# A hybrid decoder layer on one core: ordering edges for the less urgent work, four weight units split again in every tile, and the first rests on the vector engine

## The chip, the cores and the metric

The kernel runs on one core of one Trainium2 chip. The metric is the device time of one execution in microseconds; the time before is the median of three executions. Beside them one execution was profiled, and every duration below comes from that one. "Lands" means that a transfer has completed: the profile shows for each transfer when it was issued and, for most, when it landed.

## The reference, cut to what matters

The layer normalises x (2048 rows of 1024), projects it with one wide matrix, runs three kinds of head on the result, gates them, projects back, normalises and adds x.

```python
h = rms_norm(x, pre_norm_g)
proj = h @ w_in                      # 2816 columns
a_u, a_v, sq, sk, sv, mq, z = jnp.split(proj, split_at, axis=-1)
y_a = chunked_spatial_gating(gelu(a_u), gelu(a_v), ...)      # chunks of 128 rows
y_b = sliding_window_attention(sq, sk, sv, attn_sinks, rel_bias)
mk, mv = jnp.split(rms_norm(mem, mem_norm_g) @ w_mem_kv, 2, axis=-1)
y_c = memory_cross_attention(mq, mk, mv)                     # 256 memory rows
y = concatenate([y_a, y_b, y_c], axis=-1) * silu(z)
x = x + rms_norm(y @ w_out, post_norm_g)
```

Everything is float32. The kernel keeps that precision on TensorE by splitting each operand into a rounded high part and the rest, and summing three products (high by high, high by rest, rest by high).

## The kernel before, in words

**Split.** The function `split(hi, lo, src)` is the pair of instructions that the whole change is about: ScalarE (ACT) rounds `src` into `hi`, then VectorE (DVE), or for some weights GpSimd (POOL), writes the rest `src - hi` into `lo`. It is used on weights, on the normalised input and on attention probabilities.

**Tiles and units.** The 2048 rows are worked in four tiles of 512 (t = 0 to 3). In each tile TensorE (PE) runs through 22 weight units of 1024 rows by 128 columns (34 loads in all with the memory projection), 24 matmuls of 128x512 each: four units V (0 to 3), SV (4), K (5), two Q (6, 7), two MQ (8, 9), then the gate units Z (10 to 17) and U (18 to 21). A unit stands in a tile `whl` (high parts and rests, 1 MB, four buffers). Its raw weights come into `wraw` (512 KB, three buffers); the same three buffers also hold `wo_...` and `ya_...` blocks for the output projection. Once a unit has been split, it can be stored to a DRAM tensor `split_d`, and later tiles then load the ready 1 MB from there in place of loading and splitting. The table `stored_at` says in which tile a unit is stored: before, the V units are split in tiles 0 and 1 and stored in tile 1; SV, K and Q are split in tiles 0, 1 and 2 and stored in tile 2; all others are stored in tile 0.

**The end of a tile.** While PE runs the last units of tile t, the next tile's input is made: `make_h` scales a 128x512 block of x (`xj` or `xk`) on DVE and splits it into `hT`, eight blocks k = 0 to 7 in all. Unit V0 needs blocks 0 and 1, V1 blocks 2 and 3, and so on. `next_stats` squares x on ACT (`xs`) for the norm. In the same stretch the eight memory-attention pieces (named c_h_cc) end: PE transposes probabilities into `tp_c`, `split` turns them into `pT_c`, PE multiplies them into `o_c`, ACT copies half of it to `oh_c` and DVE adds both into `OC`. The gates run through `sc_z`, `Z_z`, `e_u`, `G_u` and `a`.

**What sets the order.** PE's order and that of the queue that issues the transfers (SP) are written out by hand. The orders of ACT, DVE and POOL are chosen at build time by a scheduler from its own estimate; on the chip each engine then works strictly in that order, so whatever stands behind a waiting instruction waits too. `tc.issue_after(x)` adds an edge: what is inside comes behind x on its engine. Before, `make_h`, the squares and the pieces in `aside` stand behind the latest exponentials and products of an attention piece (`late["exp"]`, `late["product"]`). In tile 3 `first_sums` reads four `ya` blocks (named 11, 21, 22 and 12), combines them and stores two sums `sd_S`.

**PSUM.** Attention pieces and the gating product `sg` share four buffers (`ps_t`): PE can begin a new one only when an earlier one has been read.

Of the kernel before, what the change touches and what calls it, by code (L numbers as in the profile page):

```python
# [11 lines left out]
AF = mybir.ActivationFunctionType  # L12
ALU = mybir.AluOpType
AX = mybir.AxisListType

P = 128
# [3 lines left out]
TS = 512  # L20
NT = SEQ // TS
# [4 lines left out]
GELU_C = math.sqrt(2.0 / math.pi)  # L26
# [4 lines left out]
U_V, U_SV, U_K, U_Q, U_MQ, U_Z, U_U, U_O, U_MK, U_MV = 0, 4, 5, 6, 8, 10, 18, 22, 30, 32  # L31
# [16 lines left out]
def kernel(  # L48
# [16 lines left out]
    nc = tc.nc  # L65
# [16 lines left out]
    def f32(ap):  # L82
        return ap.bitcast(F32)
# [1 line left out]

    aside = []

    def split(hi, lo, src, lo_engine=None):
        nc.scalar.copy(hi, src)  # L89
        (lo_engine or nc.vector).tensor_tensor(lo, src, f32(hi), ALU.subtract)  # L90


    order = []
# [33 lines left out]
    def split_unit(i):  # L127
        u, t = order[i]
        w = wp.tile([P, 2, D], F32R, tag="whl", name=f"whl_{t}_{u}")
        ready[u, t] = w  # L130
        if i not in raws:
            nc.sync.dma_start(f32(w), wo_d[u][t] if u in wo_d else split_d[u])
            return
        raw = raws.pop(i)
        if t == 0 and u in BEHIND:

            aside.append([lambda: split(w[:, 0], w[:, 1], raw), lambda: pending.discard(u)])
            pending.add(u)
# [76 lines left out]
    def next_stats(t):  # L215

        r = {}
        parts = tiny.tile([P, 2, 4], F32, tag="ss2", name=f"ss2_{t}")  # L220

        def load(n):
            i, c = divmod(n, 2)
            r[n] = sp.tile([P, TS], F32, tag="xk", name=f"xs_{t}_{n}", bufs=2)
            rows = x[t * TS : (t + 1) * TS].rearrange("(p i) d -> p i d", i=4)
            nc.sync.dma_start(r[n], rows[:, i, c * 512 : c * 512 + 512])

        def square(n):
            i, c = divmod(n, 2)

            with tc.issue_after(late["exp"].ins):
                nc.scalar.activation(r[n], r[n], AF.Square, accum_out=parts[:, c, i : i + 1])
# [30 lines left out]
    def first_h(xk, k):  # L263

        g = g_pre[:, k : k + 1]
        hT = hTs[0]
        nc.scalar.mul(hT[:, 0, k, :], xk, g)
        nc.vector.scalar_tensor_tensor(hT[:, 1, k, :], xk, g, f32(hT[:, 0, k, :]), ALU.mult, ALU.subtract)  # L268


# [10 lines left out]

    def make_h(t, k):
        hT, xk = hTs[t % 2], raw_x.pop(k)

        with tc.issue_after(late["exp"].ins), tc.issue_after(late["product"].ins):
            nc.vector.scalar_tensor_tensor(xk, xk, g_pre[:, k : k + 1], late["bcs", t], ALU.mult, ALU.mult)
            split(hT[:, 0, k, :], hT[:, 1, k, :], xk)

# [159 lines left out]


    def queue_aside(scalar, vector):  # L450
        late["product"] = vector
        with tc.issue_after(scalar.ins), tc.issue_after(vector.ins):
            for f in aside.pop(0) if aside else ():
                f()

    def window_unit(t, c, S, O, done):
# [25 lines left out]
            nc.vector.tensor_tensor(Lc[:, hs, :P], L[:, :, 0:P], L[:, :, P:], ALU.max)  # L482
        nc.vector.tensor_reduce(nm, Lc[:, :, : P + 1], axis=AX.X, op=ALU.max, negate=True)  # L483
        for h in range(4):
            last = late["exp"] = nc.scalar.activation(Lc[:, h, : P + 1], Lc[:, h, : P + 1], AF.Exp, bias=nm[:, h : h + 1],  # L485
                                        accum_out=den[:, h : h + 1])
        nc.vector.reciprocal(den, den)
        queue_aside(last, nc.vector.tensor_tensor(Lc[:, :, :P], Lc[:, :, :P],
# [3 lines left out]
        for h in range(4):  # L492
            nc.tensor.transpose(tp[:, h, :], Lc[:, h, :P], ident)
        own = sp.tile([P, 2, 4, P], F32R, tag="pT", name=f"po_{tag}")
        split(own[:, 0], own[:, 1], tp)
        if not first:

            prev = sp.tile([P, 2, 4, P], F32R, tag="pT", name=f"pp_{tag}")
# [20 lines left out]
    def memory_unit(t, h, cc, S, O, done):  # L519

        tag = f"c{t}_{h}_{cc}"
        lg = ps_t.tile([P, 2, 256], F32, tag="t", name=f"l_{tag}")
        for e in range(2):
            q0 = (2 * cc + e) * P
            for s in range(2):
                nc.tensor.matmul(lg[:, e, :], S[:, h % 2, q0 : q0 + P], MK[:, h, s, :],
                                 start=(s == 0), stop=(s == 1))
        p = sp.tile([P, 2, 256], F32, tag="L", name=f"L_{tag}", bufs=4)
        nm = tiny.tile([P, 2], F32, tag="nm", name=f"nm_{tag}", bufs=4)
        den = tiny.tile([P, 2], F32, tag="den", name=f"den_{tag}", bufs=4)  # L530
        nc.vector.tensor_reduce(nm, lg, axis=AX.X, op=ALU.max, negate=True)  # L531
        if t == 0:
            nc.vector.tensor_tensor(nm, nm, late["rstd"][:, 2 * cc : 2 * cc + 2], ALU.mult)
        for e in range(2):
            scale = late["rstd"][:, 2 * cc + e : 2 * cc + e + 1] if t == 0 else 1.0
            last = late["exp"] = nc.scalar.activation(p[:, e, :], lg[:, e, :], AF.Exp, bias=nm[:, e : e + 1], scale=scale,  # L536
                                        accum_out=den[:, e : e + 1])
        nc.vector.reciprocal(den, den)
        queue_aside(last, nc.vector.tensor_tensor(p, p, den[:, :, None].broadcast_to([P, 2, 256]), ALU.mult))
        yield  # L540
        tp = ps_t.tile([P, 2, 256], F32, tag="t", name=f"tp_{tag}")
        for j in range(2):
            for e in range(2):
                nc.tensor.transpose(tp[:, j, e * P : (e + 1) * P], p[:, e, j * P : (j + 1) * P], ident)
        pT = sp.tile([P, 2, 2, 256], F32R, tag="pT", name=f"pT_{tag}")
        split(pT[:, 0], pT[:, 1], tp)
        yield
        o = ps_t.tile([P, 256], F32, tag="t", name=f"o_{tag}")
        for n, (s, j) in enumerate(((0, 0), (0, 1), (1, 0), (1, 1))):
            nc.tensor.matmul(o, MV[:, j, h].rearrange("p a b -> p (a b)"), pT[:, s, j, :], start=(n == 0), stop=(n == 3))  # L550
        oh = sp.tile([64, 256], F32, tag="oh", name=f"oh_{tag}", bufs=1)
        nc.scalar.copy(oh, o[64:128, :])
        r0 = 64 * (h % 2)
        nc.vector.tensor_tensor(O()[r0 : r0 + 64, h // 2, 2 * cc * P : 2 * (cc + 1) * P], o[0:64, :], oh, ALU.add)
        done()

    def gelu2(ps, tag, out_tag, bufs):

        e = sp.tile([P, TS], F32, tag="e", name=f"e_{tag}", bufs=3)
        nc.scalar.activation(e, ps, AF.Square, scale=math.sqrt(GELU_A))  # L560
        nc.vector.scalar_tensor_tensor(e, e, 1.0, ps, ALU.add, ALU.mult)
        nc.scalar.activation(e, e, AF.Tanh, scale=GELU_C)
        G = sp.tile([P, TS], F32, tag=out_tag, name=f"G_{tag}", bufs=bufs)
        nc.vector.scalar_tensor_tensor(G, e, 1.0, ps, ALU.add, ALU.mult)
        return G

    def silu2(ps, tag, out_tag, bufs):

        G = sp.tile([P, TS], F32, tag=out_tag, name=f"Z_{tag}", bufs=bufs)
        nc.scalar.activation(G, ps, AF.Tanh, scale=0.5)  # L570
        nc.vector.scalar_tensor_tensor(G, G, 1.0, ps, ALU.add, ALU.mult)
        return G


# [657 lines left out]
```

## Time and profile before

| | |
|---|---|
| median of 3 executions | 775.2 us (772.15 to 775.22) |
| profiled execution | 776.51 us, of which 774.7 us are the span from its first to its last instruction |
| mean granted TensorE clock | 0.991 |
| PE busy | 758.9 us (98%) |
| DVE, ACT, POOL busy | 565.4, 394.0, 119.8 us |
| bytes moved | 200 MB, mean 259 GB/s |

The times of PE's matmuls overlap, since they are pipelined: the step from one start to the next is what counts, 0.227 us for a 128x512 one when nothing is late. So a busy share of 98% doesn't say that PE lost only 2%: it can be busy and slow. A row of the timeline merges like instructions in a run; its first number is the start in us, its second the time from the first start to the last end, and brackets hold the idle time before it and what ended that.

### The profile page before, as it was taken

The page shows a single profiled execution, that of the slowest core. Times are in us where ns is not written, and L with a number is a line of the kernel's source. Part 1 is how long each engine was busy: PE and PEld are TensorE (multiplying, and loading weights), DVE is VectorE, ACT ScalarE, POOL GpSimd, SP SyncE. Part 2 cuts the span into 40 slices and gives each one's busy share as a digit, 9 for nine tenths or more (in the row PEclk, how much of TensorE's full clock was granted, in tenths as well). Part 3 has the DMA queues.
Part 4 walks back from the last instruction along what each step waited for, and adds up shares of the span by engine and source line. Part 5 has one row for each costly group of instructions (what it writes and reads, how often), then busy time and mean ns, then how long its engine had stood idle before and what let it go on. Part 6 is the DMA issues. An engine that isn't in the chain of part 4 may idle for free. (4 is left out here: it accounts for less than half of the span.)

```text
span 774.7 us, 10625 instructions
## 1 busy us (share of the span) xinstructions
PE 758.9 (98%) x3764; PEld 639.3 (83%) x3764; DVE 565.4 (73%) x1064; ACT 394.0 (51%) x877; POOL 119.8 (15%) x125
## 2 busy tenths in 40 slices
PE   9999999989999999999999999999999999999995
PEld 7878988868888888888878888888888888888884
DVE  6496899885748889854589796647986415885787
ACT  7786776633645656246365552544444233443441
POOL 4555221000202300001023000101310000020012
PEclk9999999989999999999999999999999999999998
DMA  8856388768377898737999988774474699937618
GB/s 328 299 185 243 130 304 312 255 218 325 137 272 272 278 316 313 276 135 222 349 348 298 332 281 326 263 281 162 137 227 157 217 383 399 379 111 274 245 47 306
DMA packets 54709, 200.27 MB, mean 259 GB/s; under 512 B 5595, under 2 KB 6144, under 8 KB 44416
## 3 DMA queue, kind: packets, MB, share of 16 engines
q1 hardware_dynamic: 54128, 198.99, 72.3%
q8 instruction: 30, 0.49, 0.3%
q10 hardware_dynamic: 528, 0.59, 0.2%
q14 instruction: 23, 0.19, 0.1%
HBM read 142.93 MB, written 56.64 MB: 258 GB/s over the span
## 5 line engine op out<-in xcount | busy, mean ns | idle before, releaser
L301 PE MATMUL g_z<-hT,whl 128*128 128x512 f32 x768 | 195.3, 398 | 0.0
L301 PEld LDWEIGHTS g_z<-hT,whl 128*128 128x128 f32 x768 | 139.5, 190 | 25.3
L301 PE MATMUL g_u<-hT,whl 128*128 128x512 f32 x384 | 97.7, 396 | 0.0
L719 PE MATMUL v<-whl,hT 128*128 128x512 f32 x384 | 89.1, 392 | 0.4 <-DVE hT L268 0.3
L719 PEld LDWEIGHTS v<-whl,hT 128*128 128x128 f32 x384 | 72.1, 189 | 16.6 <-DVE hT L268 0.8
L301 PEld LDWEIGHTS g_u<-hT,whl 128*128 128x128 f32 x384 | 69.2, 188 | 12.7
L89 ACT CAST whl<-wraw 128x1024 fp32r<-128x1024 f32 (+1 forms) x39 | 39.9, 1026 | 35.7 <-DMA wraw<-in_wst 10.3
L173 POOL TENSOR_TENSOR rsr_v<-rsa_v,mhalf 128x4 f32<-128x4 f32 x16 | 16.8, 1056 | 223.3 <-DVE mv L744 202.7
L301 PE MATMUL g_q<-hT,whl 128*128 128x512 f32 x192 | 45.9, 394 | 0.0
L500 POOL TENSOR_SCALAR_AFFINE_SELECT pp_b<-po_b 128x512 fp32r<-128x512 f32 x30 | 20.8, 694 | 157.3 <-ACT po_b L89 157.3
L301 PE MATMUL g_mq<-hT,whl 128*128 128x512 f32 x192 | 44.7, 389 | 0.0
L1083 PE MATMUL Y_S<-hT,yop_S 128*128 128x512 f32 x192 | 44.2, 389 | 0.0
L1083 PE MATMUL Y<-hT,yop 128*128 128x512 f32 x192 | 43.8, 389 | 0.0
L988 POOL TENSOR_TENSOR r<-a,mhalf 128x1 f32<-128x1 f32 x16 | 13.5, 845 | 191.2 <-DVE a L986 185.1
L1083 PEld LDWEIGHTS Y<-hT,yop 128*128 128x128 f32 x192 | 36.0, 188 | 7.5
L1083 PEld LDWEIGHTS Y_S<-hT,yop_S 128*128 128x128 f32 x192 | 36.0, 188 | 7.5
L90 POOL TENSOR_TENSOR whl<-wraw,whl 128x1024 fp32r<-128x1024 f32 x16 | 38.6, 2417 | 23.2 <-ACT whl L89 23.1
L301 PEld LDWEIGHTS g_q<-hT,whl 128*128 128x128 f32 x192 | 35.7, 188 | 7.8 <-issue 0.5
L301 PEld LDWEIGHTS g_mq<-hT,whl 128*128 128x128 f32 x192 | 35.8, 188 | 7.3
L90 DVE TENSOR_TENSOR whl<-wraw,whl 128x1024 fp32r<-128x1024 f32 (+1 forms) x23 | 26.9, 1173 | 16.7 <-ACT whl L89 16.6
L536 ACT ACTIVATE L_c<-l_c,nm_c 128x256 f32<-128x256 f32 x48 | 22.4, 472 | 28.4 <-DVE nm_c L531 28.4
L485 ACT ACTIVATE Lc_b<-Lc_b,nm_b 128x129 f32<-128x129 f32 x64 | 25.0, 394 | 18.0 <-DVE nm_b L483 17.9
(211 smaller groups left out, 1468.6 us busy)
## 6 DMA issues: line engine op xcount, KB each, us to landing
whl<-split_d SPq DMA_DIRECT2D x54, 1024.0 KB, 6.2
split_d<-whl SPq DMA_DIRECT2D x22, 1024.0 KB, 8.1
wraw<-in_wst SPq DMA_DIRECT2D x37, 512.0 KB, 6.1
hT<-wo_B SPq DMA_DIRECT2D x10, 1024.0 KB, 8.8
wo_T<-hT SPq DMA_DIRECT2D x8, 1024.0 KB, 6.3
xr<-in_x SPq DMA_DIRECT2D x16, 512.0 KB, 9.4
y<-yd SPq DMA_DIRECT2D x7, 1024.0 KB, 12.0
xj<-in_xT SPq DMA_DIRECT2D x12, 512.0 KB, 5.4
```

The source lines that it names most:

```text
L89: nc.scalar.copy(hi, src)
L90: (lo_engine or nc.vector).tensor_tensor(lo, src, f32(hi), ALU.subtract)
L173: nc.gpsimd.tensor_tensor(r, a, mhalf[:, :c], ALU.pow)
L301: nc.tensor.matmul(ps, w[:, wi, k * P : (k + 1) * P], hT[:, hi, k, :], start=(n == 0), stop=(n == 3 * KC - 1))
L485: last = late["exp"] = nc.scalar.activation(Lc[:, h, : P + 1], Lc[:, h, : P + 1], AF.Exp, bias=nm[:, h : h + 1], accum_out=den[:, h : h + 1])
L500: nc.gpsimd.affine_select(prev[:, s], f32(own[:, s]), [[0, 4], [-1, P]], ALU.is_gt, 0.0, base=0, channel_multiplier=1)
L536: last = late["exp"] = nc.scalar.activation(p[:, e, :], lg[:, e, :], AF.Exp, bias=nm[:, e : e + 1], scale=scale, accum_out=den[:, e : e + 1])
L719: nc.tensor.matmul(vps[i], hT[:, hi, 2 * j + kk, i * P : (i + 1) * P], w[:, wi, kk * 512 : (kk + 1) * 512], start=(j == 0 and (hi, wi, kk) ...
L988: nc.gpsimd.tensor_tensor(r, a, mhalf2[:, 0:1], ALU.pow)
L1083: nc.tensor.matmul(banks[m], a(s, k)[:, m * P : (m + 1) * P], w(v, k), start=first and n == 0, stop=n == 11, skip_group_check=not first)
```

## The change: what it does

It has five parts.

1. A dictionary `given` holds the urgent ACT and DVE instructions given last: the attention exponentials and products as before, and now also the `pT` and `po` splits, the adds of `oh_c` into `OC`, and the last steps of the gates (`gelu2`, `silu2`). `behind_given()` puts what it wraps behind both. It now wraps the squares, `make_h`, and (new) the splits of V0, V1 and V2 for tile 1 (`LATE`). In `MAKES`, the first four blocks of tile 1's input are asked for one slot later.
2. SV, K and Q get `stored_at` = 4, a tile that doesn't exist: they are split in all four tiles and never stored. In tile 2 that takes away four 1 MB stores. In tile 3 four 1 MB loads become four 512 KB raw loads and four splits.
3. The rests of units V1, V2 and V3 in tile 0 go from POOL to DVE.
4. The first block of `hT` in tile 0 is rounded in two halves, one on ACT and one on DVE.
5. Nothing changes in the arithmetic, in PE's order or after the four tiles.

```diff
+LATE = ((U_V, 1), (U_V + 1, 1), (U_V + 2, 1))
-MAKES = ((59, 61, 63, 65, -28, -28, -24, -24), (50, 52, 55, 57, -28, -28, -24, -24))
+MAKES = ((60, 62, 64, 66, -28, -28, -24, -24), (50, 52, 55, 57, -28, -28, -24, -24))
...
-    def split(hi, lo, src, lo_engine=None):
-        nc.scalar.copy(hi, src)
-        (lo_engine or nc.vector).tensor_tensor(lo, src, f32(hi), ALU.subtract)
+    def split(hi, lo, src, lo_engine=None, urgent=False):
+        a = nc.scalar.copy(hi, src)
+        b = (lo_engine or nc.vector).tensor_tensor(lo, src, f32(hi), ALU.subtract)
+        if urgent:
+            given["scalar"], given["vector"] = a, b
+    given = {}
+    def behind_given():
+        edges = ExitStack()
+        for ins in given.values():
+            edges.enter_context(tc.issue_after(ins.ins))
+        return edges
...
-    stored_at = {u: 1 if u < U_SV else 2 if u < U_MQ else 0 for u in range(U_O)}
+    stored_at = {u: 1 if u < U_SV else NT if u < U_MQ else 0 for u in range(U_O)}
...
-            split(w[:, 0, c], w[:, 1, c], raw[:, c], nc.vector if i > 16 or i == 0 else nc.gpsimd)
+            if i == 0:
+                split(w[:, 0, c], w[:, 1, c], raw[:, c])
+                continue
+            with behind_given() if (u, t) in LATE else ExitStack():
+                split(w[:, 0, c], w[:, 1, c], raw[:, c], nc.gpsimd if 4 <= i <= 16 else nc.vector)
...
-            with tc.issue_after(late["exp"].ins):
+            with behind_given():
                 nc.scalar.activation(r[n], r[n], AF.Square, accum_out=parts[:, c, i : i + 1])
...
-        nc.scalar.mul(hT[:, 0, k, :], xk, g)
+        if k == 0:
+            nc.scalar.mul(hT[:, 0, k, 0:256], xk[:, 0:256], g)
+            nc.vector.tensor_scalar(hT[:, 0, k, 256:TS], xk[:, 256:TS], g, None, ALU.mult)
+        else:
+            nc.scalar.mul(hT[:, 0, k, :], xk, g)
...
-        with tc.issue_after(late["exp"].ins), tc.issue_after(late["product"].ins):
+        with behind_given():
             nc.vector.scalar_tensor_tensor(xk, xk, g_pre[:, k : k + 1], late["bcs", t], ALU.mult, ALU.mult)
             split(hT[:, 0, k, :], hT[:, 1, k, :], xk)
...
-        split(pT[:, 0], pT[:, 1], tp)
+        split(pT[:, 0], pT[:, 1], tp, urgent=True)
```

The built programs show what the scheduler makes of it. First DVE at the end of tile 0, behind the product of the last attention piece, before (`xj` and `xk` scalings and `hT` rests are the next tile's input, `whl` rests are weights, `pT_c_3_0` is the rest of piece c_3_0's probabilities, `OC` with `o_c_2_0` is the add that frees PSUM):

```order
L539 TENSOR_TENSOR L_c_3_1_1623<-L_c_3_1_1623,den_c_3_1_1625 128x512
L286 SCALAR_TENSOR_TENSOR xj_0_1455<-xj_0_1455,colt,bcs_1586 128x512 x2
L286 SCALAR_TENSOR_TENSOR xj_2_1503<-xj_2_1503,colt,bcs_1586 128x512 x2
L286 SCALAR_TENSOR_TENSOR xk_4_1602<-xk_4_1602,colt,bcs_1586 128x512
L286 SCALAR_TENSOR_TENSOR xk_5_1656<-xk_5_1656,colt,bcs_1586 128x512
L90 TENSOR_TENSOR whl_13_1575<-wraw_13_1492,whl_13_1575 128x1024
L90 TENSOR_TENSOR whl_0_1666<-wraw_0_1576,whl_0_1666 128x1024
L554 TENSOR_TENSOR OC_1464<-o_c_1_1_1658,oh_c_1_1_1663 64x256
L564 SCALAR_TENSOR_TENSOR G_u_2_1646<-e_u_2_1642,sc_u_2_1640 128x512
L90 TENSOR_TENSOR pT_c_2_1_1684<-tp_c_2_1_1679,pT_c_2_1_1684 128x512
...
L90 TENSOR_TENSOR pT_c_3_0_1727<-tp_c_3_0_1722,pT_c_3_0_1727 128x512
L554 TENSOR_TENSOR OC_1464<-o_c_2_0_1699,oh_c_2_0_1704 64x256
```

And now:

```order
L559 TENSOR_TENSOR L_c_3_1_1624<-L_c_3_1_1624,den_c_3_1_1626 128x512
L92 TENSOR_TENSOR whl_13_1576<-wraw_13_1493,whl_13_1576 128x1024
L574 TENSOR_TENSOR OC_1465<-o_c_1_1_1659,oh_c_1_1_1664 64x256
L92 TENSOR_TENSOR whl_0_1667<-wraw_0_1577,whl_0_1667 128x1024
L823 SCALAR_TENSOR_TENSOR Z_z_6_1475<-OC_1465,Z_z_6_1475 128x512
L584 SCALAR_TENSOR_TENSOR G_u_2_1647<-e_u_2_1643,sc_u_2_1641 128x512
L92 TENSOR_TENSOR pT_c_2_1_1685<-tp_c_2_1_1680,pT_c_2_1_1685 128x512
L574 TENSOR_TENSOR OC_1465<-o_c_2_0_1700,oh_c_2_0_1705 64x256
L328 TENSOR_TENSOR sc_z_2_1714<-g_z_2_1673,bcs_489 128x512
L883 TENSOR_TENSOR a_2_1654<-a_2_1654,G_u_2_1647 128x512
L92 TENSOR_TENSOR pT_c_3_0_1725<-tp_c_3_0_1720,pT_c_3_0_1725 128x512
L306 SCALAR_TENSOR_TENSOR xj_0_1456<-xj_0_1456,colt,bcs_1587 128x512
```

The six scalings that stood in front of `pT_c_2_1` and `pT_c_3_0`, and the four to six `hT` rests and the rest of `whl_1` between them, now stand behind both. At the ends of tiles 1 and 2 the same happens on a smaller scale.

Second, SP at the start of tile 3. Before, the four units were loads of ready splits and depended on PE only:

```order
L132 DMA whl_4_4731<-split_d 128x2048
L584 DMA yd<-a_3_4617 128x512
L132 DMA whl_5_4766<-split_d 128x2048
L132 DMA whl_6_4798<-split_d 128x2048
L636 DMA ya_0_4828<-yd 128x2x512
L584 DMA sd_S_89<-ya_0_4723 128x2x512
L132 DMA whl_7_4940<-split_d 128x2048
L584 DMA sd_S_90<-ya_0_4828 128x2x512
L132 DMA whl_8_4972<-split_d 128x2048
```

Now (`ya_0_4726` is block 22, `ya_0_4836` is block 12):

```order
L656 DMA ya_0_4726<-yd 128x2x512
L604 DMA yd<-Z_z_6_4312 128x512
L604 DMA yd<-Z_z_7_4393 128x512
L138 DMA wraw_5_4733<-in_wst 128x1024
L604 DMA yd<-a_3_4614 128x512
L138 DMA wraw_6_4771<-in_wst 128x1024
L138 DMA wraw_7_4806<-in_wst 128x1024
L656 DMA ya_0_4836<-yd 128x2x512
L604 DMA sd_S_89<-ya_0_4722 128x2x512
L604 DMA sd_S_90<-ya_0_4836 128x2x512
L146 DMA whl_8_4981<-split_d 128x2048
```

The four raw loads share three buffers with the `ya` blocks. By the semaphores of the built program, block 22 waits for the rest of unit 4, the load of unit 5 for block 22's combination, that of unit 6 for the rest of unit 5, that of unit 7 for the rest of unit 6, block 12 for the rest of unit 7, the second store for block 12's combination; and unit 8 stands behind them all on SP.

More of the change, by code (lines that the diff above doesn't have):

```diff
@@ L450, in queue_aside @@
     def queue_aside(scalar, vector):
-        late["product"] = vector
+        given["scalar"], given["vector"] = scalar, vector
         with tc.issue_after(scalar.ins), tc.issue_after(vector.ins):
@@ L484, in window_unit @@
         for h in range(4):
-            last = late["exp"] = nc.scalar.activation(Lc[:, h, : P + 1], Lc[:, h, : P + 1], AF.Exp, bias=nm[:, h : h + 1],
+            last = nc.scalar.activation(Lc[:, h, : P + 1], Lc[:, h, : P + 1], AF.Exp, bias=nm[:, h : h + 1],
                                         accum_out=den[:, h : h + 1])
@@ L494, in window_unit @@
         own = sp.tile([P, 2, 4, P], F32R, tag="pT", name=f"po_{tag}")
-        split(own[:, 0], own[:, 1], tp)
+        split(own[:, 0], own[:, 1], tp, urgent=True)
         if not first:
@@ L535, in memory_unit @@
             scale = late["rstd"][:, 2 * cc + e : 2 * cc + e + 1] if t == 0 else 1.0
-            last = late["exp"] = nc.scalar.activation(p[:, e, :], lg[:, e, :], AF.Exp, bias=nm[:, e : e + 1], scale=scale,
+            last = nc.scalar.activation(p[:, e, :], lg[:, e, :], AF.Exp, bias=nm[:, e : e + 1], scale=scale,
                                         accum_out=den[:, e : e + 1])
@@ L551, in memory_unit @@
         oh = sp.tile([64, 256], F32, tag="oh", name=f"oh_{tag}", bufs=1)
-        nc.scalar.copy(oh, o[64:128, :])
+        given["scalar"] = nc.scalar.copy(oh, o[64:128, :])
         r0 = 64 * (h % 2)
-        nc.vector.tensor_tensor(O()[r0 : r0 + 64, h // 2, 2 * cc * P : 2 * (cc + 1) * P], o[0:64, :], oh, ALU.add)
+        given["vector"] = nc.vector.tensor_tensor(O()[r0 : r0 + 64, h // 2, 2 * cc * P : 2 * (cc + 1) * P], o[0:64, :], oh, ALU.add)
         done()
@@ L561, in gelu2 @@
         nc.vector.scalar_tensor_tensor(e, e, 1.0, ps, ALU.add, ALU.mult)
-        nc.scalar.activation(e, e, AF.Tanh, scale=GELU_C)
+        given["scalar"] = nc.scalar.activation(e, e, AF.Tanh, scale=GELU_C)
         G = sp.tile([P, TS], F32, tag=out_tag, name=f"G_{tag}", bufs=bufs)
-        nc.vector.scalar_tensor_tensor(G, e, 1.0, ps, ALU.add, ALU.mult)
+        given["vector"] = nc.vector.scalar_tensor_tensor(G, e, 1.0, ps, ALU.add, ALU.mult)
         return G
@@ L569, in silu2 @@
         G = sp.tile([P, TS], F32, tag=out_tag, name=f"Z_{tag}", bufs=bufs)
-        nc.scalar.activation(G, ps, AF.Tanh, scale=0.5)
-        nc.vector.scalar_tensor_tensor(G, G, 1.0, ps, ALU.add, ALU.mult)
+        given["scalar"] = nc.scalar.activation(G, ps, AF.Tanh, scale=0.5)
+        given["vector"] = nc.vector.scalar_tensor_tensor(G, G, 1.0, ps, ALU.add, ALU.mult)
         return G
```

## The prediction

> **What bounds the kernel now.** I read the page's first part, then PE's waits and its timeline at each end of a tile, since PE's order is the same in both kernels: the change can only alter what PE waits for.
>
> ```profile
> PE 758.9 (98%) x3764; PEld 639.3 (83%) x3764; DVE 565.4 (73%) x1064; ACT 394.0 (51%) x877; POOL 119.8 (15%) x125
> ```
>
> PE bounds the kernel, and of its 774.7 us span nothing but its stalls and slow stretches can go. The worst is the end of tile 0 (waits of PE from 146 to 176 us, then PE's timeline there):
>
> ```profile
> PE sg L858 <- DVE pT_c L90: 2.8, 1, 2.8
> ...
> 157.25 0.40 PE L550 MATMUL o_c<-pT_c,MV 128*128 128x256 f32 x2
> 157.88 0.50 PE L550 MATMUL o_c<-pT_c,MV 128*128 128x256 f32 x2 [0.24 <-DVE pT_c L90]
> ...
> 159.96 1.63 PE L301 MATMUL g_u<-hT,whl 128*128 128x512 f32 x6
> 164.42 2.08 PE L858 MATMUL sg<-wsp,vhat 128*128 128x128 f32 x8 [2.83 <-DVE pT_c L90]
> 166.15 2.91 PE L301 MATMUL g_z<-hT,whl 128*128 128x512 f32 x6
> 168.86 1.05 PE L550 MATMUL o_c<-pT_c,MV 128*128 128x256 f32 x4
> ...
> 174.65 21.95 PE L719 MATMUL v<-whl,hT 128*128 128x512 f32 x96
> ```
>
> The end of tile 2 runs the same work nearly undisturbed and serves as the yardstick:
>
> ```profile
> 456.44 0.40 PE L550 MATMUL o_c<-pT_c,MV 128*128 128x256 f32 x2
> 457.34 0.50 PE L550 MATMUL o_c<-pT_c,MV 128*128 128x256 f32 x2 [0.51 <-DVE pT_c L90]
> ...
> 460.43 1.05 PE L858 MATMUL sg<-wsp,vhat 128*128 128x128 f32 x8
> 461.32 0.60 PE L544 MATMUL tp_c<-ident,L_c 128*128 128x128 f32 x4
> 461.67 1.64 PE L301 MATMUL g_z<-hT,whl 128*128 128x512 f32 x6
> 463.14 0.65 PE L550 MATMUL o_c<-pT_c,MV 128*128 128x256 f32 x4
> 463.63 4.26 PE L301 MATMUL g_z<-hT,whl 128*128 128x512 f32 x18
> 467.73 0.64 PE L550 MATMUL o_c<-pT_c,MV 128*128 128x256 f32 x4
> 468.20 2.00 PE L719 MATMUL v<-whl,hT 128*128 128x512 f32 x8
> ```
>
> A 512-column matmul steps by (467.73 - 463.63)/18 = 0.228 us, a 256-column one by (468.20 - 467.73)/4 = 0.12. Six gate matmuls take 1.47 (461.67 to 463.14), but after the wait in tile 0 they take 2.71 (166.15 to 168.86): PE runs at half speed for some 4 us behind the wait.
>
> The Trainium skill, "TensorE: Matmul & The Clock Gate", section "Part 1: The HAM clock gate (the "warmup" mystery)", says that an idle window of about 3.4 us, which runs freely, halves PE's clock until a busy window has passed. The trace roughly agrees: 3.1 us of wait brought the slow stretch.
>
> **The change part by part.** *Ordering edges, end of tile 0.* PE's `sg` wants a PSUM buffer that DVE frees with `pT_c` and the add into `OC`. DVE shows why they are late:
>
> ```profile
> 149.72 2.73 DVE L286 SCALAR_TENSOR_TENSOR xj<-xj,colt,bcs 128x512 f32<-128x512 f32 x4
> 152.37 1.41 DVE L286 SCALAR_TENSOR_TENSOR xk<-xk,colt,bcs 128x512 f32<-128x512 f32 x2
> 153.69 2.36 DVE L90 TENSOR_TENSOR whl<-wraw,whl 128x1024 fp32r<-128x1024 f32 x2
> ...
> 157.14 0.68 DVE L90 TENSOR_TENSOR pT_c<-tp_c,pT_c 128x512 fp32r<-128x512 f32 x1
> 157.74 1.89 DVE L90 TENSOR_TENSOR hT<-xj,hT 128x512 fp32r<-128x512 f32 x3
> ...
> 163.69 0.68 DVE L90 TENSOR_TENSOR pT_c<-tp_c,pT_c 128x512 fp32r<-128x512 f32 x1
> 164.29 0.41 DVE L554 TENSOR_TENSOR OC<-o_c,oh_c 64x256 f32<-64x256 f32 x1
> ```
>
> Now the six scalings (4.0 us) stand behind both. The first `pT_c` then ends near 154, `OC` near 155 and `pT_c_3_0` near 157, where PE asks for the buffer at 159.96 + 6 x 0.227 = 161.3. So the wait goes with some 4 us to spare, and the slow stretch with it: 164.42 - 161.32 = 3.1, and `sg` to `v` 10.23 (164.42 to 174.65) against 7.77 - 0.35 for the four `tp_c` = 7.42 (460.43 to 468.20; `tp_c` from 461.32 to 461.67): 2.8. The `o_c` at 157.88 comes 0.63 behind the pair at 157.25, where two steps of 0.12 are due, and lasts 0.10 longer than that pair: 0.5. Together **6.4**. What is late next: the scalings, rests and `whl_1` (4.0 + 8 x 0.61 + 1.2 = 10.1 us) now run behind 157, mixed with gate work; adding DVE's rows in the new order puts the rests of blocks 2 and 3 at 170.1, 4 and 5 at 177.8, 6 and 7 at 179.6. With `v` starting at 168.4, their units' rest products begin at 175.6, 181.1 and 184.8 (two blocks are 24 matmuls, 5.45 us, and the first eight of them need no rest). The smallest cover is 3.4 us.
>
> *The same edges, ends of tiles 1 and 2.* At 457.34 the `o_c` pair comes 0.90 behind the one before, 0.67 too late, and lasts 0.10 longer: 0.77. Tile 1 shows the same:
>
> ```profile
> 309.68 0.50 PE L550 MATMUL o_c<-pT_c,MV 128*128 128x256 f32 x2 [0.48 <-DVE pT_c L90]
> ```
>
> Taken as 0.74; together **1.5** (bounds 0 and 1.5). The moved rests have at least 5 us of cover there.
>
> *No stores of units 4 to 7.* In tile 2 SP issues four 1 MB stores between 347 and 375, and the squares' input comes late behind them:
>
> ```profile
> 375.25 0.91 SPq L226 DMA_DIRECT2D xs<-in_x  x2
> ...
> 383.24 0.63 ACT L232 ACTIVATE xs<-xs 128x512 f32<-128x512 f32 x1 [4.57 <-DMA xs<-in_x]
> ...
> 391.12 0.28 PE L510 MATMUL o_b<-pp_b,SV 128*128 128x256 f32 x1
> ...
> 393.85 0.60 PE L493 MATMUL tp_b<-ident,Lc_b 128*128 128x128 f32 x4
> ```
>
> ACT stands still 4.57 us, the probabilities behind it come late, and the eight `o_b` matmuls from 391.12 to 393.85 take 2.73 instead of 0.96: **1.8** goes (bounds 0 and 1.8).
>
> *The price of that, tile 3.* Four 1 MB loads become raw loads with casts and rests. ACT and DVE have room in sum, but the three `wraw` buffers make a chain across tile 3's start, each link a transfer of 512 KB, a cast and a rest (page; then a single transfer of each size, the 1 MB one with a store just ahead):
>
> ```profile
> wraw<-in_wst SPq DMA_DIRECT2D x37, 512.0 KB, 6.1
> L89 ACT CAST whl<-wraw 128x1024 fp32r<-128x1024 f32 (+1 forms) x39 | 39.9, 1026 | 35.7 <-DMA wraw<-in_wst 10.3
> ...
> ya<-yd SPq DMA_DIRECT2D x1, 512.0 KB, 3.8
> whl<-split_d SPq DMA_DIRECT2D x1, 1024.0 KB, 5.9
> ```
>
> Let V be the start of `v` in tile 3 (468.20 before). DVE's last gate product can start at V + 0.33, when ACT's tanh ends, and then does it (0.6), an add into `OC` (0.3), four scalings (2.7), two gate steps (1.2), four `hT` rests (2.4) and the rest of unit 4 (1.2), by the rows from 149.72 on: V + 8.8. Then block 22 (3.8), its combination (2 x 0.63), three links for units 5, 6 and 7 (3.8 + 1.0 + 1.2 = 6.0 each), block 12 (3.8) and its combination, V + 37.0; issuing the second store 0.4, and unit 8 behind it 5.9: V + 43.3. PE wants it here:
>
> ```profile
> 467.93 0.60 ACT L570 ACTIVATE Z_z<-g_z 128x512 f32<-128x512 f32 x1 [3.20 <-PE g_z L301]
> ...
> 512.24 5.60 PE L301 MATMUL g_mq<-hT,whl 128*128 128x512 f32 x24
> ```
>
> that is V + 44.0. Ten hand-overs of about 0.1 use up the 0.7 left. I take **0.4** of new wait: it is nearest to these rows, which are transfers that ran nearly alone, as they would here, where each waits for the one ahead. Bounds: 0 and, at the page's 6.1 for every transfer, 12 (a rival below). Units 5, 6 and 7 themselves come 6 us or more before PE wants them.
>
> *The start.* The halved first block and the first rests on DVE touch this:
>
> ```profile
> 5.34 6.36 PE L719 MATMUL v<-whl,hT 128*128 128x512 f32 x24
> 15.75 13.89 PE L719 MATMUL v<-whl,hT 128*128 128x512 f32 x60 [0.35 <-DVE hT L268]
> ...
> L90 POOL TENSOR_TENSOR whl<-wraw,whl 128x1024 fp32r<-128x1024 f32 x3 | 7.5, 2488 | 8.6 <-ACT whl L89 8.6
> L268 DVE SCALAR_TENSOR_TENSOR hT<-xj,colt,hT 128x512 fp32r<-128x512 f32 x6 | 9.6, 1664 | 2.7 <-ACT hT L267 2.7
> ```
>
> The first `v` can start 0.24 earlier, where PE's warming matmuls end (5.1). At 15.75 PE waits 0.35 for an `hT` rest; the wait at 457.34 cost 0.26 more than its bracket of 0.51, so I take 0.6 here too. DVE's six cost 1664 ns on average while POOL subtracts, though the like scalings at 149.72 cost 0.68; with POOL idle they should fall to that, and the three rests cost DVE 1.2 each. **0.9** goes (bounds -0.6, if DVE is then the later one, and 0.9).
>
> The Trainium skill, "Perfetto Trace Analysis", section "Optimizing Scalar/DVE Operations", warns that POOL and DVE share a read port, so that moving work between them may not help. By it the start would give 0.24 only and the forecast be 0.6 longer; the 1664 against 0.68 agrees with the sharing, but says that moving helps.
>
> **Sum:** 6.4 + 1.5 + 1.8 + 0.9 - 0.4 = 10.2, less 0.1 for roundings upward: 10.1. From the profiled 776.5 that is 766.4; that execution lay 1.3 above the median of 775.2 (runs 772.15 to 775.22), so a median between 765.1 and 766.4: **765.7**.
>
> **Rivals.** *R1, the buffer chain is late by a few us.* Each of its five small transfers needs only 0.5 us more for unit 8 to come 3 us late. For it speaks that transfers behind others took 6.1 in the median; against it that here each starts alone. A 3 us wait brings 2.8 of slow clock as at tile 0's end: gain 10.5 - 5.8 = 4.7, 770.5 to 771.8.
>
> The section on the clock gate of the Trainium skill's page "TensorE: Matmul & The Clock Gate" lets a wait of that length pass at full clock if it straddles two windows; by it R1 would be 2.8 shorter, and no row of a 3 us wait here shows that.
>
> *R2, the wait at tile 0's end only moves.* If the displaced rests are over 3.4 us later than added up, PE waits in `v` instead, and the 5.9 comes back: 771. For it: DVE is busy without a gap there; against it: the cover.
>
> *R3, slower.* The chain's five 512 KB transfers take the page's 6.1: 5 x 2.3 = 11.5 more, unit 8 0.3 more, so PE waits 11.5 + 0.3 + 0.4 = 12.2 for `mq` plus 2.8 of slow clock: 15.0 - 10.5 = 4.5 slower, 779.7. It turns the sign from about 1.5 us more per transfer on. Against it: nothing else stands in the queue then but two `yd` stores and one load.
>
> *R4, the change doesn't do what it says:* PE's releaser at 161 was not DVE's order but something that stays late. Then only the start and tile 2 gain, 2.3 net: 773.
>
> **How the numbers follow.** Forecast 0.70 (its own range 763.5 to 768.5: the bounds of the 1.5, 1.8 and 0.9 and a chain up to 1.5 us late), R1 0.13, R2 0.08, R4 0.05, R3 0.04. The range 762.0 to 771.5 takes in R2 and most of R1; its low end allows the runs' own spread of 3 us. 0.5% (3.9 us) is about what a measurement here can tell from no change, so faster means below 771.3: the forecast, nearly all of R2 and some of R1, 0.83; same 0.13 (R4, the rest of R1 and R2); slower 0.04 (R3).
>
> **What would show it.** Right: PE's wait of `sg` for `pT_c` in tile 0 is gone, six `g_z` matmuls behind it take 1.4 to 1.5, `v` of tile 1 starts near 167.5 on a clock that starts 0.9 earlier; the `o_b` row near 391 steps at 0.12; no `split_d` stores of units 4 to 7. Wrong: a wait of `v` for `hT` in tile 1 (R2), `g_mq` in tile 3 waiting for `whl` over 1 us (R1; over 10, R3), a wait of the first `v` units for `whl` on DVE.

## The result, and the profile after

The changed kernel takes 769.7 us (median of 7 runs, 767.4 to 770.9) against 775.2 before (7 runs, 770.8 to 777.5): a ratio of 0.9936 with an interval of 0.991 to 0.9963. That is faster by 5.5 us, or 0.6%; the prediction had said 765.7, 9.5 us less, with a range of 762.0 to 771.5. The profiled execution took 769.78 us, 767.9 of them its span, so 6.7 less than the profiled one of before, where the prediction's sum had 10.1.

The page's busy times and PE's waits over the whole span (who waited, for what, in total, times, longest):

```profile
PE 753.9 (98%) x3764; PEld 635.7 (83%) x3764; DVE 567.4 (74%) x1072; ACT 398.0 (52%) x881; POOL 112.9 (15%) x122
...
PE warm L213 <- POOL ident masks.py:199: 1.5, 1, 1.5
PE svt L804 <- DVE sc_sv L328: 1.3, 1, 1.3
PE g_mq L321 <- DMA whl<-split_d: 1.3, 1, 1.3
PE bc L274 <- POOL rsr_x L191: 0.5, 1, 0.5
```

The waits of `sg`, `o_c`, `o_b` and `v` that the prediction counted are all gone. Two of over 1 us have come: `svt` in tile 0, which the prediction doesn't mention, and `g_mq` in tile 3, which it took at 0.4. A third of 0.5, `bc` in tile 0, isn't in the prediction either.

The end of tile 0, PE's timeline and then DVE's:

```profile
158.10 0.64 PE L570 MATMUL o_c<-pT_c,MV 128*128 128x256 f32 x4
161.79 1.05 PE L878 MATMUL sg<-wsp,vhat 128*128 128x128 f32 x8
162.60 1.63 PE L321 MATMUL g_z<-hT,whl 128*128 128x512 f32 x6
164.06 0.65 PE L570 MATMUL o_c<-pT_c,MV 128*128 128x256 f32 x4
164.55 4.26 PE L321 MATMUL g_z<-hT,whl 128*128 128x512 f32 x18
168.65 0.64 PE L570 MATMUL o_c<-pT_c,MV 128*128 128x256 f32 x4
169.12 7.22 PE L739 MATMUL v<-whl,hT 128*128 128x512 f32 x31
...
154.76 0.68 DVE L92 TENSOR_TENSOR pT_c<-tp_c,pT_c 128x512 fp32r<-128x512 f32 x1
155.36 0.41 DVE L574 TENSOR_TENSOR OC<-o_c,oh_c 64x256 f32<-64x256 f32 x1
155.69 0.68 DVE L328 TENSOR_TENSOR sc_z<-g_z,bcs 128x512 f32<-128x512 f32 x1
156.29 0.68 DVE L883 TENSOR_TENSOR a<-a,G_u 128x512 f32<-128x512 f32 x1
156.89 0.68 DVE L92 TENSOR_TENSOR pT_c<-tp_c,pT_c 128x512 fp32r<-128x512 f32 x1
157.49 0.74 DVE L306 SCALAR_TENSOR_TENSOR xj<-xj,colt,bcs 128x512 f32<-128x512 f32 x1
```

`sg` follows the gate's matmuls without a pause, and the six `g_z` behind it take 1.46 us (162.60 to 164.06) where they took 2.71. The first `pT_c` ends at 155.4, `OC` at 155.8 and the second `pT_c` at 157.6; the scalings of `xj` come behind them. From `sg` to `v` it is 7.33 us; before it was 10.23.

The eight `o_b` of tile 2, where ACT no longer waits for the squares' input:

```profile
384.84 0.28 PE L530 MATMUL o_b<-pp_b,SV 128*128 128x256 f32 x1
384.95 0.28 PE L530 MATMUL o_b<-po_b,SV 128*128 128x256 f32 x1
...
385.80 0.38 PE L513 MATMUL tp_b<-ident,Lc_b 128*128 128x128 f32 x2
```

They take 0.96 us instead of 2.73. The two places where time was lost (PE's timeline again, and ACT's last square of x at the start):

```profile
32.79 1.16 PE L274 MATMUL bc<-ident,rsr_x 128*128 128x128 f32 x8 [0.47 <-POOL rsr_x L191]
44.83 0.66 PE L804 MATMUL svt<-ident,sc_sv 128*128 128x128 f32 x4 [1.33 <-DVE sc_sv L328]
...
29.29 1.06 ACT L226 ACTIVATE xp<-xp 128x1024 f32<-128x1024 f32 x1 [0.17 <-DMA xp<-in_x]
...
504.91 5.70 PE L321 MATMUL g_mq<-hT,whl 128*128 128x512 f32 x24 [1.32 <-DMA whl<-split_d]
```

Since PE runs the same 3764 matmuls in the same order, the start of each in one trace can be set against the other. The table gives how the distance to the trace of before changes over each stage, up to the start of the next; minus is time won. What a wait costs behind its bracket is in its stage. The last column is a second execution of the unaltered changed kernel (the run "again" below).

| stage | predicted | changed kernel | again |
|---|---|---|---|
| start to behind `svt` (50 us) | -0.9 | +0.9 | -0.4 |
| end of tile 0 | -6.4 | -6.4 | -6.3 |
| `o_c` at the end of tile 1 | -0.7 | -0.7 | -0.6 |
| `o_b` in tile 2 | -1.8 | -1.8 | -1.7 |
| `o_c` at the end of tile 2 | -0.8 | -0.8 | -0.7 |
| `mq` in tile 3 | +0.4 | +1.6 | +1.7 |
| behind that, with the last output | 0 | +0.5 | +0.5 |
| span | -10.1 | -6.8 | -7.5 |

The +0.9 of the first row is made of 1.4 won by 18 us, 0.7 lost at `bc` and 1.5 lost at `svt`. Both of these hang on the statistics of x, which were late in this execution: its last square began at 29.29 us, that of before at 28.10.

### The profile page after: what moved, and what is told of

Same layout as the page of the kernel before. It is cut to its first block, busy times and chain, and to the rows that moved or that the text cites. A ratio compares the mean times of both kernels' runs of the same rounds, so it can differ in the third digit from the quotient of the medians.

```text
span 767.9 us, 10627 instructions
## 1 busy us (share of the span) xinstructions
PE 753.9 (98%) x3764; PEld 635.7 (83%) x3764; DVE 567.4 (74%) x1072; ACT 398.0 (52%) x881; POOL 112.9 (15%) x122
## 5 line engine op out<-in xcount | busy, mean ns | idle before, releaser
L91 ACT CAST whl<-wraw 128x1024 fp32r<-128x1024 f32 (+1 forms) x43 | 44.2, 1028 | 40.2 <-DMA wraw<-in_wst 22.4
L92 DVE TENSOR_TENSOR whl<-wraw,whl 128x1024 fp32r<-128x1024 f32 (+1 forms) x30 | 35.9, 1198 | 19.5 <-ACT whl L91 19.4
L92 POOL TENSOR_TENSOR whl<-wraw,whl 128x1024 fp32r<-128x1024 f32 x13 | 31.1, 2402 | 31.8 <-ACT whl L91 31.7
L979 DVE TENSOR_TENSOR yop<-y,yop 128x1024 fp32r<-128x1024 f32 x12 | 14.6, 1219 | 24.0 <-DMA y<-yd 15.0
```

The source lines that it names most:

```text
L91: a = nc.scalar.copy(hi, src)
L92: b = (lo_engine or nc.vector).tensor_tensor(lo, src, f32(hi), ALU.subtract)
L979: nc.vector.tensor_tensor(w[:, 1, ks], yraw[name, p][:, ks], f32(w[:, 0, ks]), ALU.subtract)
```

## The experiments

The theory after the two traces: the gains lie in separate stages and are as predicted; what was lost is (a) a chain from the statistics of x that doesn't get earlier with PE, and (b) the chain through the raw buffers. The rivals are that the parts depend on one another, and that one of the losses belongs to that one execution.

The runs were taken in three series, and each ratio is to the kernel before in the same series (median 774.4, 775.3 and 774.8 us). Across series only the ratios can be compared; the changed kernel has 0.9936 and, run again, 0.9929.

### The ordering edges alone

The changed kernel with parts 2, 3 and 4 undone.

```diff
-    stored_at = {u: 1 if u < U_SV else NT if u < U_MQ else 0 for u in range(U_O)}
+    stored_at = {u: 1 if u < U_SV else 2 if u < U_MQ else 0 for u in range(U_O)}
...
-                split(w[:, 0, c], w[:, 1, c], raw[:, c], nc.gpsimd if 4 <= i <= 16 else nc.vector)
+                split(w[:, 0, c], w[:, 1, c], raw[:, c], nc.gpsimd if i <= 16 else nc.vector)
...
-        if k == 0:
-            nc.scalar.mul(hT[:, 0, k, 0:256], xk[:, 0:256], g)
-            nc.vector.tensor_scalar(hT[:, 0, k, 256:TS], xk[:, 256:TS], g, None, ALU.mult)
-        else:
-            nc.scalar.mul(hT[:, 0, k, :], xk, g)
+        nc.scalar.mul(hT[:, 0, k, :], xk, g)
```

> The changed kernel with parts 2, 3 and 4 undone (units 4 to 7 stored in tile 2 again, rests of V1 to V3 on POOL, first block whole): only the ordering edges are left. Theory (the gains lie in separate stages and add up): PE's wait of sg at the end of tile 0 and the half clock behind it go (6.0 us by the changed kernel's trace), and the o_c waits near 158, 310 and 457 (0.5, 0.65, 0.8): 7.9 us less than before, a ratio of 0.990. The 4.6 us wait of ACT in tile 2 and the slow o_b stay. Rival (the end of tile 0 is only better because the start or the lighter tile 2 gave room): less than 5 us gained, and a wait of v or sg at 160 to 175 left. For the start: the last square of x on ACT begins at 28.1 as before if the 1.2 us delay of the changed kernel comes from the change of the start, anywhere between 28 and 29.5 if it is the spread of the transfers.

Measured: 769.6 us, ratio 0.9932 (0.9908 to 0.9956), span 768.7. The end of tile 0 is as in the changed kernel (`sg` to `v` 7.33, PE 6.4 us nearer than at `svt`), and so are the `o_c` waits. So the gain there comes from the edges, and needs neither the start nor the lighter tile 2. But only 6.0 of the 7.9 us came, since a new wait stands in tile 2 (PE, then ACT):

```profile
394.13 1.13 PE L874 MATMUL sg<-wsp,vhat 128*128 128x128 f32 x8 [1.67 <-DVE OB L531]
...
376.17 0.63 ACT L249 ACTIVATE xs<-xs 128x512 f32<-128x512 f32 x1 [4.58 <-DMA xs<-in_x]
...
388.82 0.63 ACT L249 ACTIVATE xs<-xs 128x512 f32<-128x512 f32 x1 [5.36 <-DMA xs<-in_x]
389.36 0.19 ACT L249 ACTIVATION_READ_ACCUMULATOR xs<-xs 128x1 f32 x1
389.45 0.39 ACT L501 ACTIVATE Lc_b<-Lc_b,nm_b 128x129 f32<-128x129 f32 x1
```

A square that waits 5.36 us for its input stands ahead of the exponentials of an attention piece. In the kernel before, the exponentials at this place went first. PE waited 1.7 us there and lost 1.9. Neither theory nor rival had this.

### The units alone

The kernel before with part 2 alone:

```diff
-    stored_at = {u: 1 if u < U_SV else 2 if u < U_MQ else 0 for u in range(U_O)}
+    stored_at = {u: 1 if u < U_SV else NT if u < U_MQ else 0 for u in range(U_O)}
```

> The kernel before with part 2 alone (units 4 to 7 split in all four tiles, never stored). Theory: the eight o_b matmuls near 391 fall from 2.7 to 1.0 us, since ACT's 4.6 us wait for the squares' input goes (-1.8), and mq in tile 3 waits 1 to 1.5 us for unit 8 behind the chain through the raw buffers (+1.4): in sum -0.4, no difference to be measured. Rival (the mq wait comes from the edges, which put the hT rests late ahead of the rest of unit 4): mq doesn't wait, -1.8. The wait of sg at 161 stays in both.

Measured: 772.9 us, ratio 0.9979 (0.9966 to 0.9993). The `o_b` stretch gave its 1.8 us. `mq` didn't wait (PE, and ACT at the start of the chain):

```profile
508.96 3.34 PE L301 MATMUL g_mq<-hT,whl 128*128 128x512 f32 x14
...
470.84 1.05 ACT L89 CAST whl<-wraw 128x1024 fp32r<-128x1024 f32 x1 [3.66 <-DMA wraw<-in_wst]
...
471.93 1.23 DVE L90 TENSOR_TENSOR whl<-wraw,whl 128x1024 fp32r<-128x1024 f32 x1 [2.08 <-ACT whl L89]
```

The rival holds, though by little: unit 8 landed 0.2 us ahead of PE in this one profile. The ten runs agree with it (1.5 us less than before, where the rival said 1.8 and the theory 0.4). With V = 464.92 for the start of `v` in tile 3, the rest of unit 4 ends at V + 8.2 here. In the changed kernel (V = 459.39) it ends at V + 10.2:

```profile
459.49 0.42 SPq L138 DMA_DIRECT2D wraw<-in_wst  x1
...
467.32 1.05 ACT L91 CAST whl<-wraw 128x1024 fp32r<-128x1024 f32 x1 [3.00 <-DMA wraw<-in_wst]
...
468.40 1.22 DVE L92 TENSOR_TENSOR whl<-wraw,whl 128x1024 fp32r<-128x1024 f32 x1 [1.13 <-ACT whl L91]
```

In both, the cast waits for the transfer: DVE's tail ahead of it, on which the prediction started its chain, isn't what ends last. The raw weights are issued at V + 0.1 in both and cast from V + 5.9 here, from V + 7.9 there. So between these two profiles the chain is 2 us later through the transfers. An x block (`xj`) that was issued at V - 4.4 was there at V - 0.3 in the kernel before; with the edges it is issued at V - 6.7 and lands at V + 1.8, together with a store of `yd` and a 1 MB load issued within 1 us. That these three are in one another's way is argued, not shown. Seven profiles have the edges and part 2. In five of them the `xj` block landed at V + 1.8 to V + 2.4, and the cast began at V + 7.7 to V + 8.3; in the other two it landed at V - 0.1 and V + 1.1, and the cast began at V + 6.0. So the transfer isn't late in every execution. In those two DVE's tail is what ends last, as the prediction had it, and unit 4's rest ends at V + 9.0, still 0.8 later than without the edges. One of them is the run "svt later" below (V = 457.69; ACT, then DVE):

```profile
463.66 1.05 ACT L91 CAST whl<-wraw 128x1024 fp32r<-128x1024 f32 x1 [1.04 <-DMA wraw<-in_wst]
...
465.49 1.22 DVE L92 TENSOR_TENSOR whl<-wraw,whl 128x1024 fp32r<-128x1024 f32 x1
```

A second thing shows. PE's wait for `sg` at the end of tile 0 is still there, with the same 2.83 us, but what follows is shorter than in the profile of before:

```profile
164.16 2.08 PE L858 MATMUL sg<-wsp,vhat 128*128 128x128 f32 x8 [2.83 <-DVE pT_c L90]
165.89 2.38 PE L301 MATMUL g_z<-hT,whl 128*128 128x512 f32 x6
168.10 0.64 PE L550 MATMUL o_c<-pT_c,MV 128*128 128x256 f32 x4
...
173.16 3.14 PE L719 MATMUL v<-whl,hT 128*128 128x512 f32 x13
```

From `sg` to `v` it is 9.00 us, against 10.23 before and 7.33 undisturbed. The same wait cost 2.9 us of slow clock in one execution and 1.7 in another.

### The start alone

The kernel before with parts 3 and 4 alone.

```diff
-            split(w[:, 0, c], w[:, 1, c], raw[:, c], nc.vector if i > 16 or i == 0 else nc.gpsimd)
+            split(w[:, 0, c], w[:, 1, c], raw[:, c], nc.gpsimd if 4 <= i <= 16 else nc.vector if i else nc.vector)
...
-        nc.scalar.mul(hT[:, 0, k, :], xk, g)
+        if k == 0:
+            nc.scalar.mul(hT[:, 0, k, 0:256], xk[:, 0:256], g)
+            nc.vector.tensor_scalar(hT[:, 0, k, 256:TS], xk[:, 256:TS], g, None, ALU.mult)
+        else:
+            nc.scalar.mul(hT[:, 0, k, :], xk, g)
```

> The kernel before with parts 3 and 4 alone (first rests on DVE, first block halved). Theory (what is won at the start is taken back at 44 us, because the transposes svt there wait for a chain from the statistics of x that doesn't get earlier): PE is 1.0 to 1.3 us earlier at 15 us, svt waits 0.9 to 2 us for DVE's sc_sv, and PE is no earlier than before at 45 us (0 to 0.9 us later): ratio 1.000 to 1.001. Rival (the svt wait comes from another part): PE keeps 0.9 to 1.3 us to the end, svt waits under 0.3. If the statistics are late because of this part, the last square of x begins near 29.3 here and at 28.1 with the edges alone; if that is the transfers' spread, the two don't differ by the kernel.

Measured: 775.0 us, ratio 1.0013 (0.9997 to 1.0029): no gain. But not for the reason expected. PE was only 0.4 us earlier at 15 us, not 1.0 to 1.3, and kept 0.3 at `svt`, which didn't wait. The last square began at 28.1. So the 1.2 us by which the statistics were late in the changed kernel's profile isn't caused by this part. And `sg` to `v` behind the old wait took 9.05 us here.

### The changed kernel again

Unaltered.

> The changed kernel once more, unaltered, to see which of its two new waits belong to the kernel and which to that one execution. In six profiled executions of six kernels so far the last square of x began at 28.4 or earlier on ACT, in the changed kernel's alone at 29.3. Theory A (a late transfer of that execution, on top of a chain that has only 0.2 us to spare): the last square begins at 27.8 to 28.5, svt waits 0.2 to 0.6 rather than 1.3, and PE stands 0.4 to 1.0 us better at 45 us; the mq wait in tile 3 stays at 1 to 1.5. Theory B (the kernel's own): both waits at 1.2 to 1.4 again.

Measured: 769.8 us, ratio 0.9929 (0.9908 to 0.9949), span of the profile 767.1. Theory A holds, and by more than it said: the last square began at 27.7 and `svt` has no wait left, where 27.8 to 28.5 and 0.2 to 0.6 were expected (ACT, PE):

```profile
27.70 1.06 ACT L226 ACTIVATE xp<-xp 128x1024 f32<-128x1024 f32 x1 [0.39 <-DMA xp<-in_x]
...
43.46 0.61 PE L804 MATMUL svt<-ident,sc_sv 128*128 128x128 f32 x4
...
504.13 5.71 PE L321 MATMUL g_mq<-hT,whl 128*128 128x512 f32 x24 [1.47 <-DMA whl<-split_d]
```

The wait of `mq` is there again.

### svt later in PE's order

```diff
-            if i == (t == 0):
+            if i == (2 if t == 0 else 0):
```

> The changed kernel with svt of tile 0 six matmuls later in PE's order, and nothing else. Theory: PE no longer waits there (under 0.3 us), the mq wait of 1 to 1.5 us stays; 0.4 to 1.6 us less than the changed kernel, by how late the statistics come in the execution. Rival (K's or SV's next use is late in its place): a new wait of 0.5 or more between 45 and 60 us and no gain.

Measured: 768.5 us (four runs: 767.3, 769.6, 770.0, 767.5), against 769.8 for the changed kernel in the same series. In the profile PE doesn't wait there, nothing waits in its place, and `mq` waits 1.30. The runs' spread is as large as what is looked for, so the time alone decides nothing; the trace agrees with the theory.

### The load of unit 8 ahead of a store

```diff
-                store_later(sums_d[name][k : k + 2].rearrange("k p n -> p k n"), src, 10 if k else 4)
+                store_later(sums_d[name][k : k + 2].rearrange("k p n -> p k n"), src, 10 if k else 8)
```

> The changed kernel with the second sum's store of tile 3 asked for later, so that the load of unit 8 stands ahead of it, and nothing else. Theory: mq doesn't wait for unit 8, which lands 2 us or more ahead of PE; 1.2 to 1.5 us less than the changed kernel. Rival (the queue behind it slips and unit 9 or 14 is late instead): PE waits 0.5 us or more for another unit between 505 and 525.

Measured: 766.7 us (four runs, 766.5 to 767.5), ratio 0.9893 (0.9864 to 0.9922), against 769.8 for the changed kernel in the same series. SP's queue in the changed kernel, and then here with PE's next wait:

```profile
492.93 0.38 SPq L656 DMA_DIRECT2D ya<-yd  x1
493.35 5.31 SPq L604 DMA_DIRECT2D sd_S<-ya  x2
498.76 1.30 SPq L146 DMA_DIRECT2D whl<-split_d  x2
```

```profile
491.80 0.46 SPq L604 DMA_DIRECT2D sd_S<-ya  x1
492.36 0.42 SPq L146 DMA_DIRECT2D whl<-split_d  x1
497.17 0.36 SPq L604 DMA_DIRECT2D sd_S<-ya  x1
...
501.77 5.60 PE L321 MATMUL g_mq<-hT,whl 128*128 128x512 f32 x24
...
508.60 0.50 PE L495 MATMUL l_b<-KK,S_q 128*128 128x256 f32 x2 [0.52 <-DVE S_q L466]
```

In the changed kernel the second store waits on SP for the combination of block 12, and the load of unit 8 behind it. Counted from V (457.73 here), the load goes 4.7 us earlier, unit 8 lands 1.6 us ahead of PE, and `mq` doesn't wait. The rival named a wait of 0.5 us or more for another unit. None came, but `l_b` waits 0.5 for DVE's `S_q`, and PE loses 0.8 there by the comparison of starts. So the chain costs what stands behind it in the queue, and a store that nobody is in a hurry for held up a load that PE needs. The medians differ by 3.1 us, and the waits of `mq` in four profiles of kernels that have them are 1.3 to 1.9 us (1.32, 1.47, 1.30, 1.86). PE lost 1.6 at `mq` in the changed kernel's trace, and 0.8 at `l_b` here; so the traces show 0.8 us of the 3.1 at this place, and the rest lies elsewhere or in the spread of executions.

### Both

The two edits above together.

> The changed kernel with two waits taken away: svt in tile 0 stands six matmuls later in PE's order (behind 18 of the Q unit's 24), and the store of the second sum in tile 3 is asked for later, so that the load of unit 8 stands ahead of it on SP and no longer behind the combination of block 12. Theory: the svt wait (1.33 by its bracket, 1.6 with the pipeline) falls to 0.1 to 0.4, the mq wait (1.3) goes: 2.5 to 3 us less than the changed kernel, near 767. Rival (the waits move to the next one that needs the same: K's or Q's products, l_b, later loads): under 1 us gained, with a new wait of PE within 15 us behind either place.

Measured: 766.8 us (four runs, 766.6 to 767.3), ratio 0.9897 (0.9873 to 0.9921), a ratio lower by 0.003 to 0.004 (some 3 us) than that of the changed kernel, as expected. PE's wait of 0.5 us for `l_b`, which the rival had in mind, is there again. But the load alone gives the same time, so it isn't the sum of two edits.

### The squares as before

The edges alone, but with the squares behind the latest exponentials only:

```diff
-            with behind_given():
+            with tc.issue_after(late["exp"].ins):
                 nc.scalar.activation(r[n], r[n], AF.Square, accum_out=parts[:, c, i : i + 1])
```

> The kernel with the ordering edges alone (units 4 to 7 stored in tile 2, start as before), but with the squares behind the latest exponentials only, as in the kernel before. It is to tell why the edges alone lost 1.7 us in tile 2, where PE waited for sg on DVE's OB add. Theory (a square that waits 5.4 us for its input stands on ACT ahead of an attention piece's exponentials, since the new rule ties it to whatever was given last; the four stores make that input late): that wait of sg is gone, about 1.7 us less than with all the edges, while the slow o_b stays. Rival (the rest of the edges shifts DVE): the wait of sg near 394 stays at 1 us or more.

Measured: 767.6 us, ratio 0.9905 (0.9869 to 0.9941). The wait of `sg` in tile 2 is gone, as the theory said. The ratio is 0.003 (2 us) below that of the edges alone; the two intervals overlap, so it is the trace that decides. The kernel is no slower than the whole change. The same edit in the changed kernel, where the stores are gone:

> The changed kernel with the squares of x behind the latest exponentials only, as in the kernel before. With the edges alone the new rule for the squares cost 1.7 us in tile 2, where their input comes late behind four stores. Theory (the rule is harmful only while the stores hold the input back): nothing to gain here, the trace agrees with the changed kernel's to 0.4 us behind tile 0, mq waits 1.3 to 1.5 us again, 769 to 770. Rival (the squares' edges cost something in every tile): 1.5 to 2.5 us less, with some wait of PE or ACT gone that the changed kernel has.

Measured: 768.6 us, ratio 0.9917 (0.9897 to 0.9937), span 767.3; `mq` waits 1.86 and `svt` 1.1, and behind tile 0 the trace has no stage that differs from the changed kernel's by over 0.6 us. So the new rule for the squares costs nothing once their input is early. With the load moved as well:

> The changed kernel with the load of unit 8 ahead of the second sum's store and the squares as before. Theory: as with the load moved alone, 766.5 to 767, since the squares matter only with the stores. Rival (both edits count): 765 or less.

Measured: 766.4 us (four runs, 765.4 to 767.8), ratio 0.9892 (0.987 to 0.9914), the lowest here, but not to be told from 766.7.

## Why the prediction was right in sign and too large

**End of tile 0: right.** 6.4 predicted, 6.4 measured, and the run with the edges alone gives it to them. DVE's new order put the `pT_c` and `OC` where the prediction had added them up (154, 155 and 157; by the trace 155.4, 155.8, 157.6, in a run that was 0.9 later). No wait of `v` for `hT` came: R2 is out, and so are R4 and R3.

**Ends of tiles 1 and 2, and the `o_b` of tile 2: right**, 0.7, 0.8 and 1.8 against 0.74, 0.77 and 1.8. The cause given for the last, four stores that hold SP, is shown by the units alone.

**Tile 3: the mechanism was right, the term mis-sized.** 0.4 predicted; PE waited 1.3 to 1.9 us in four profiles and lost 1.6 to 2.1, so it is R1's mechanism at half its size and without its slow clock. In the changed kernel the step that failed is the chain's start: "V + 8.8", worked out from DVE's tail. By the trace it is V + 10.2, because the first raw block's transfer takes until V + 7.9. The prediction gave that transfer no time of its own. From there on its steps held: 35.3 us from the end of unit 4's rest to PE's start of `mq` (469.6 to 504.9) against 34.5 and 1.0 for hand-overs. But the start isn't the whole of it. With `svt` later, unit 4's rest ends at V + 9.0, nearly as predicted, and `mq` waits 1.30 all the same; there it is unit 7's raw load that took 5.0 us, where it took 3.3 to 3.5 in the other three and the prediction had 3.8. So it is the chain's transfers that were priced too low, and which of them is late varies by execution.

**The start: mis-sized, and its cover overlooked.** 0.9 was read from one execution of before, as if its 15.75 were what that kernel always has. Kernels with the old start reached the same matmul 0.3, 0.4 and 0.4 us earlier than that (units alone, edges alone, squares as before), and those with the new start 0.2 to 1.3 earlier, 0.67 on average over eight profiles. So the two edits are worth some 0.4. DVE's rests did fall to 0.70 us once POOL was idle, as said (changed kernel, two of them):

```profile
10.84 1.41 DVE L289 SCALAR_TENSOR_TENSOR hT<-xj,colt,hT 128x512 fp32r<-128x512 f32 x2
```

But PE wasn't waiting for them by as much as it seemed. And the prediction didn't look for who waits next: `svt` hangs on a chain from the statistics of x (last square, `rsr_x`, `sc_v`, DVE's queue, `sc_sv`) that ended 0.2 us ahead of PE in the trace of before. Where PE comes earlier or the last block of x later, it waits: 1.3, 1.1, 0.5 and 0.2 us in four profiles, none in the others that have it at its old place.

**The tie to the median: wrong by about a microsecond.** The profiled execution of before lay 1.3 us above the median. The prediction took the middle of two ties, 10.1 less than that execution (766.4) and 10.1 less than the median (765.1). By the two runs that kept the wait, 1.2 us of that execution was a longer slow stretch behind `sg` (10.23 against 9.00 and 9.05), which the change takes away; an execution at the median had less to win, and 766.4 was the right tie. From 766.4 to the 769.8 of the changed kernel's profile it is then 3.4 us: 1.8 at the start, 1.2 at `mq`, 0.5 behind it, and roundings. That other executions of before differ in the same way is argued, since only one of them has a trace. The clock that the record gives for each agrees: of 37 others between 772 and 779 us, the seven with a mean granted clock of 0.991 to 0.993 took 776.0 to 778.7 us, the seven with 0.997 or more 772.3 to 774.6.

**The parts aren't independent**, which the prediction took for granted when it added them. The edges without part 2 lose 1.9 us in tile 2; part 2 without the edges has no wait of `mq` in its profile; and the edges without the squares' rule are, alone, as fast as the whole change.

## What to carry to other kernels

When urgent work is put ahead of less urgent work on an in-order engine, look at which of the pushed-back instructions can itself wait for a transfer: at its new place it holds up whatever comes behind it. When a load is replaced by a chain through shared buffers, look first at what stands behind the chain in the queue that issues it; here one store asked for four slots later took a wait of over 1 us away, and the two edits of the start together won nothing that could be measured. And a gain that is read from a single execution, at a place where a clock or a transfer varies, should be priced from several.

## What the runs showed of the hardware that was not expected

The same wait of 2.83 to 2.85 us was followed by 2.9, 1.7 and 1.7 us of slow clock in three executions (from `sg` to `v` 10.23, 9.00 and 9.05, against 7.33 without). The granted clock stood at 0.50 for 6.8 us in the first (163.7 to 170.5) and for 3.4 us in the others (164.1 to 167.5 and 164.3 to 167.7): the price came as two stretches of 3.4 us or as one. The Trainium skill, "TensorE: Matmul & The Clock Gate", section "Part 1: The HAM clock gate (the "warmup" mystery)", says that the clock falls after an idle window of about 3.4 us and that the window runs freely. The length of the stretches agrees with that, and so does a price that varies by execution; but the waits here were shorter than such a window, and the clock fell all the same. Waits of 1.1 to 1.9 us (`svt`, `mq`, `sg` in tile 2) brought no slow stretch behind them: the granted clock stayed at 1.00 around them in the profiles of the changed kernel, of `svt` later, of the squares as before in the changed kernel, and of the edges alone.

The last square of x began between 26.8 and 29.3 us over the twelve profiles, with the same loads in the same order ahead of it and no link to the old or the new start (27.6 to 28.4, and 26.8 to 29.3): 2.5 us of spread. The cast of raw weights that stands just ahead of it on ACT waits for its transfer, 3.1 us in the trace of before, 3.7 in the changed kernel's and 1.5 with `svt` later, where the square began earliest. The spread is more than all that the start's edits are worth.
